# Norm gain moved into the row transposes, small softmax work moved behind the slot table, TensorE order fixed in the route

## The chip, the cores and the metric

One core of one Trainium2 chip. The time is the device time of one execution in microseconds (us): median 3249.14 of 3 runs before the change (3241.06 to 3254.65). TensorE does the matmuls, VectorE, ScalarE and GpSimd the elementwise work, SyncE (SP) issues most DMAs. In the profile PE is TensorE, PEld its weight loads, DVE VectorE, ACT ScalarE, POOL GpSimd.

## The reference, cut to what matters

Two transformer blocks on 1024 tokens of width 1024. The first ends with a mixture of experts; the change is in its routing:

```python
h = _rms_norm(x, norm_ffn_g)                      # rows of hf
g_logits = hf @ w_group_router + b_group_router   # 4 groups
g_probs = softmax(g_logits)
g_gate, g_sel = top_k(g_probs, 1)
e_logits = (hf @ w_expert_router + b_expert_router)[chosen group]   # 8 experts
e_probs = softmax(e_logits)
e_gate, e_sel = top_k(e_probs, 2)
e_gate = e_gate / sum(e_gate)
weights = g_gate * e_gate
# each token goes to 2 of 32 experts; tokens are sorted into slots by expert
hidden = silu(xb @ w_gate[e]) * (xb @ w_up[e])    # xb = hf[tok], the rows of one block of slots
y = (hidden @ w_down[e]) * wt
```

Since the last division cancels the expert softmax's own sum, only the ratio of the two chosen exponentials and the chosen group's share of the group sum enter the weights.

## The kernel before, in words

Activations lie transposed: eight tiles `self.xs[c]` of 128 features by 1024 tokens. Products that need precision run as three passes in the fast 32-bit format (`mm3`, L114 to L116, on high and low parts split by L91 and L94); a few small ones run as plain f32 matmuls, which the hardware carries out as two instructions each (L1004, L1116), and transposes, one instruction each, against the identity matrix.

The first block's cross attention ends with `out(512)` (L735 to L742). Behind it, for each half of 512 tokens, `moe_logits` (L996) computes the norm's reciprocal root and the router's 36 logits per token (L1004, L1009, L1011, L1012), and `moe_rows` (L1015) makes token rows: for each of four blocks of 128 tokens it transposes eight 128x128 pieces (L1023) into two PSUM banks, ScalarE evicts each bank with the token's reciprocal root as scale (L1024), GpSimd multiplies the row by the norm's weights, which `grow` holds copied to all partitions (L1025), and SP writes it to `hrow` in DRAM (L1026). In the text, `moe_rows(0)` stands between the two `moe_logits`, and `moe_rows(512)` behind `route` (L1036, L1037).

`route` (L779) runs almost wholly on VectorE, with instructions of 8 to 256 elements a partition: group softmax (`softmax_small`), first maximum with its one-hot (`first_max`), the logits of the chosen group, expert softmax, two maxima, the weights `wt`, the one-hots `of`, and their sum `both`. TensorE counts positions (L812 with a strictly triangular matrix, then eight matmuls of ones, L815), VectorE picks each token's place, and `turn` (L841) turns token numbers into a slot table per expert by 16 small matmuls against one-hots of the place (L845, L847). `tix` (L832) is the table as integers. Then come expert numbers and counts for `route_rest` (L849), which is called at the third expert and treats experts with more than 112 tokens.

The experts follow: `expert_in` gathers the slots' rows from `hrow` with an indirect DMA from GpSimd (L934), which needs `tix` and all of `hrow`, transposes them (L939) and multiplies with the expert's weights (three loads of 1 MB each on SP, L1047, 12 buffers); `expert_out` makes the second product and writes it to `yrow` (L1060).

The order on each engine isn't that of the text: a planner goes through the program with simulated times and puts what is ready, earliest in the text first. So before the change rows of the second half run on TensorE ahead of the route's own matmuls. `manual_schedule(engines={PE})` makes one region's TensorE instructions issue in the order of the text; where they fall among instructions outside the region stays with the planner. `warm(n)` (L118) issues n matmuls of 512 columns whose result nobody reads; it is used elsewhere in the kernel (L1135 to L1155).

Of the kernel before, what the change touches and what calls it, by code (L numbers as in the profile page):

```python
# [22 lines left out]
P = 128  # L23
S = 1024
D = 1024
# [40 lines left out]
class K:  # L66
# [51 lines left out]
    def warm(self, n):  # L118

        c = self.c  # L120
        ps = self.ps("S", (P, S), 2)[:, 0:512].rearrange("p (r q) -> p r q", q=P)
        for _ in range(n):
            self.nc.tensor.matmul(ps, c["identr"], c["nmaskr"][:, None, :].to_broadcast([P, 4, P]), start=True, stop=True)
# [643 lines left out]
    def softmax_small(self, pool, l, n, tag):  # L767
        nc = self.nc
# [5 lines left out]
        nc.vector.tensor_reduce(mx, p, axis=AX.X, op=OP.add)  # L774
        nc.vector.reciprocal(mx, mx)
        nc.vector.tensor_tensor(p, p, mx.to_broadcast([P, NB, n]), op=OP.mult)
        return p

    def route(self, pool, rp, lg):  # L779
# [15 lines left out]
        den = self.t(rp, [P, NB, 1], tag="den")  # L795
        V.tensor_tensor(den, pk[0], pk[1], op=OP.add)
        V.reciprocal(den, den)
        wt = self.t(pool, [P, NB, 2], tag="wt")
        for k in range(2):
            V.tensor_tensor(wt[:, :, k:k + 1], pk[k], den, op=OP.mult)  # L800
            V.tensor_tensor(wt[:, :, k:k + 1], wt[:, :, k:k + 1], gg, op=OP.mult)
# [11 lines left out]
        for t in range(NB):  # L813
            n = NB - t
            nc.tensor.matmul(ps[:, (t + 1) * 32:].rearrange("p (t e) -> p t e", e=32), self.onesr, both[:, t:t + 1].to_broadcast([P, n, 32]), start=False, stop=(t == NB - 1))  # L815
        pos = ps[:, :256].rearrange("p (t e) -> p t e", e=32)
# [6 lines left out]
        for k in range(2):  # L823
# [6 lines left out]
            self.turn(rp, ps, k, places[k], cols, F32R)  # L830
        tix = self.t(pool, [CAP, 32], I32, tag="tix")
        V.tensor_copy(tix, ps)  # L832

        experts, counts = self.t(pool, [P, 2, NB], tag="experts"), self.t(pool, [P, 32], tag="counts")
        V.tensor_copy(counts, total)
        for k in range(2):
            V.scalar_tensor_tensor(experts[:, k], gv[:, :, 0], 8.0, ev[k][:, :, 0], op0=OP.mult, op1=OP.add)
# [132 lines left out]
    def moe_open(self):  # L970
# [13 lines left out]
        self.grow = self.t(hp, [P, D], tag="grow")  # L984
        nc.sync.dma_start(self.grow, a["norm_ffn_g"].partition_broadcast(P))
# [29 lines left out]
    def moe_rows(self, t0):  # L1015

        nc, hp = self.nc, self.moeh
        for i in range(4):
            row = self.t(self.moeh, [P, D], tag="row", bufs=3)
            for q in range(2):  # L1020
                tp = self.ps("T")
                for n in range(4):
                    nc.tensor.transpose(tp[:, n * P:(n + 1) * P], self.xs[4 * q + n][:, t0 + i * P:t0 + (i + 1) * P], self.c["ident"])  # L1023
# [966 lines left out]
```

## Time and profile before

| | before |
|---|---|
| median of 3 runs | 3249.14 us |
| profiled execution | 3258.15 us, its span 3255.6 us |
| mean granted TensorE clock | 0.967 of full |
| TensorE busy | 3033.3 us, 93% |
| TensorE weight loads | 2447.2 us, 75% |
| VectorE busy | 1618.8 us, 50% |
| ScalarE busy | 1449.5 us, 45% |
| GpSimd busy | 1117.5 us, 34% |
| the chain that ended last | TensorE 53%, every other engine and DMA 1% or less |

Times in the rows below are microseconds from the span's start. A timeline row gives start, length (of a merged group, from its first start to its last end), engine, line, operation, output<-inputs, sizes and count, and in brackets how long the engine had been idle and what ended that. The granted clock is a share of full speed; its two levels are 1.2 and 2.4 GHz, 0.50 and 1.00.

### The profile page before, as it was taken

To read this page: it belongs to the slowest core of one execution; us is meant where nothing else is said; L and a number is where in the kernel's file an instruction comes from. 1 tells how busy PE (TensorE), PEld (TensorE's weight loads), DVE (VectorE), ACT (ScalarE), POOL (GpSimd) and SP (SyncE) were. 2 spreads that over 40 slices of the span, in tenths; PEclk is the share of its full clock that TensorE was granted. 3 is DMA by queue.
4 is the path that set the end of the run, shared out by engine and by line. 5 is a ranking of instruction groups with operands and counts; after the bars stand their busy time and mean duration, and the time that the engine had idled before them with its cause. 6 is when DMAs were issued, how large, how long until landed. Compare 5 with 4: busy or idle time off the path is not lost.

```text
span 3255.6 us, 41825 instructions
## 1 busy us (share of the span) xinstructions
PE 3033.3 (93%) x14660; PEld 2447.2 (75%) x14660; DVE 1618.8 (50%) x3295; ACT 1449.5 (45%) x2906; POOL 1117.5 (34%) x914
## 2 busy tenths in 40 slices
PE   6999779988988999899999999999899999999999
PEld 4787657776756666677888888888777788888887
DVE  6567985577468888663445464331555311111111
ACT  4555664563537888632444453444434221121121
POOL 3334445654533433441111111112656322222221
PEclk9998878999998999999999999999999999999999
DMA  5553636422267999435453333325653211111112
GB/s 161 214 201 125 237 122 197 109 66 85 64 246 270 387 381 356 167 117 153 126 163 123 114 114 104 115 95 197 202 172 112 67 46 47 48 49 43 48 46 81
DMA packets 213003, 469.34 MB, mean 144 GB/s; under 512 B 27544, under 2 KB 69048, under 8 KB 200504
## 3 DMA queue, kind: packets, MB, share of 16 engines
q1 hardware_dynamic: 206392, 443.59, 41.2%
q0 software_dynamic: 6400, 23.07, 2.2%
q8 instruction: 116, 1.90, 0.2%
q14 instruction: 95, 0.78, 0.1%
HBM read 352.28 MB, written 113.77 MB: 143 GB/s over the span
## 4 chain that ended last, share of the span: by engine, by line
PE 53%; DMA 1%; DVE 1%; POOL 1%; ACT 1%; issue 1%; SPq 0%; ACTq 0%; POOLq 0%; DVEq 0%
PE mm L114 16%; PE mm L115 16%; PE mm L116 16%; PE T L1249 1%; PE T L1229 1%; PE S L1477 1%; POOL wlo L94 1%; PE T L1729 0%; PE mm L172 0%; PE T L1710 0%; DMA gt<-gd 0%; PE S L1571 0%; PE S L1570 0%; POOL yg L1100 0%; DMA yg<-yrow,sloti 0%
## 5 line engine op out<-in xcount | busy, mean ns | idle before, releaser
L94 POOL TENSOR_TENSOR wlo<-wraw,whi 128x512 fp32r<-128x512 f32 (+3 forms) x487 | 611.9, 1260 | 1475.7 <-ACT whi L91 1382.8
L115 PE MATMUL mm<-hl,whi 128*128 128x512 f32 (+2 forms) x1968 | 786.5, 400 | 12.0 <-DVE hl L94 6.5
L114 PE MATMUL mm<-hh,whi 128*128 128x512 f32 (+2 forms) x1968 | 787.3, 401 | 10.5 <-DVE qkl L217 2.1
L116 PE MATMUL mm<-hh,wlo 128*128 128x512 f32 (+2 forms) x1968 | 785.0, 399 | 0.0
L91 ACT CAST whi<-wraw 128x512 fp32r<-128x512 f32 (+3 forms) x487 | 287.1, 594 | 712.2 <-PE mm L115 616.8
L115 PEld LDWEIGHTS mm<-hl,whi 128*128 128x128 f32 (+2 forms) x1968 | 371.9, 189 | 100.6 <-DVE hl L94 9.8
L114 PEld LDWEIGHTS mm<-hh,whi 128*128 128x128 f32 (+2 forms) x1968 | 371.7, 189 | 99.3 <-issue 5.0
L116 PEld LDWEIGHTS mm<-hh,wlo 128*128 128x128 f32 (+2 forms) x1968 | 371.7, 189 | 83.2
L94 POOL TENSOR_TENSOR ptl<-praw,pth 128x512 fp32r<-128x512 f32 (+2 forms) x192 | 205.8, 1075 | 235.1 <-DVE pth L1239 200.0
L91 ACT CAST whi<-w 128x512 fp32r<-128x512 f32 x384 | 232.8, 624 | 49.3 <-PE mm L116 18.7
L94 DVE TENSOR_TENSOR wlo<-w,whi 128x512 fp32r<-128x512 f32 x320 | 239.2, 776 | 29.2 <-ACT whi L91 26.1
L1867 DVE TENSOR_TENSOR ffgate<-ffgate,mm 128x512 f32<-128x512 f32 x44 | 30.2, 687 | 384.4 <-PE mm L116 384.4
L1229 PE MATMUL T<-ident,p 128*128 128x128 f32 x864 | 147.4, 291 | 20.5 <-DVE p L450 7.3
L94 POOL TENSOR_TENSOR wlo<-w,whi 128x512 fp32r<-128x512 f32 x64 | 88.6, 1385 | 201.7 <-ACT whi L91 137.3
L1878 DVE TENSOR_TENSOR x<-mm,x 128x512 f32<-128x512 f32 x64 | 44.2, 692 | 199.1 <-PE mm L116 199.1
L1229 PEld LDWEIGHTS T<-ident,p 128*128 128x128 f32 x864 | 107.5, 149 | 44.5 <-ACT praw L1238 9.0
L114 PE MATMUL mm<-ah,whi 128*128 128x512 f32 x352 | 139.6, 397 | 0.3 <-DVE x L1878 0.3
L115 PE MATMUL mm<-al,whi 128*128 128x512 f32 x352 | 139.6, 396 | 0.0
L116 PE MATMUL mm<-ah,wlo 128*128 128x512 f32 x352 | 139.5, 396 | 0.0
L94 DVE TENSOR_TENSOR ptl<-T,pth 128x512 fp32r<-128x512 f32 (+2 forms) x128 | 73.2, 578 | 120.7 <-ACT pth L91 88.9
L1238 ACT COPY praw<-T 128x512 f32<-128x512 f32 (+2 forms) x192 | 90.4, 478 | 82.4 <-PE T L1229 63.5
L444 DVE CUSTOM_DVE_ANT_0 p<-S,dist 128x128 f32<-128x128 f32 (+7 forms) x128 | 94.9, 750 | 40.5 <-PE S L443 32.4
(496 smaller groups left out, 5774.4 us busy)
## 6 DMA issues: line engine op xcount, KB each, us to landing
w<-w_expert SPq DMA_DIRECT2D x96, 1024.0 KB, 10.1
wraw<-w_in SPq DMA_DIRECT2D x152, 256.0 KB, 2.8
gd<-gate SPq DMA_DIRECT2D x64, 256.0 KB, 2.0
gt<-gd SPq DMA_DIRECT2D x16, 1024.0 KB, 6.4
yrow<-y SPq DMA_DIRECT2D x32, 448.0 KB, 3.1
wraw<-w_gate SPq DMA_DIRECT2D x48, 256.0 KB, 2.5
wraw<-w_up SPq DMA_DIRECT2D x48, 256.0 KB
vd<-vs SPq DMA_DIRECT2D x18, 512.0 KB, 2.8
```

What stands on the lines that cost most here:

```text
L91: self.nc.scalar.copy(out, x)
L94: (eng or self.nc.vector).tensor_tensor(out, x, h.bitcast(F32), op=OP.subtract)
L114: self.nc.tensor.matmul(out, lh, rh, start=(i == 0), stop=False)
L115: self.nc.tensor.matmul(out, lh, rl, start=False, stop=False)
L116: self.nc.tensor.matmul(out, ll, rh, start=False, stop=(i == n - 1))
L444: V.tensor_tensor_reduce(p[:, :nk], sps[:, :nk], dist[qb], slope, 3e38, OP.add, OP.min, st[:, m:m + 1])
L1229: nc.tensor.transpose(tp[:, i * P:(i + 1) * P], p[:, (k0 + i) * P:(k0 + i + 1) * P], self.c["ident"])
L1238: nc.scalar.copy(y, src)
L1249: nc.tensor.matmul(o[:, q0:256], vs[:, kb], pt[kb // 4][:, kb % 4, q0:256], start=(pt is pth and kb == 0), stop=(pt is ptl and kb == nkb - 1))
L1477: self.nc.tensor.matmul(o, q, k[:, k0:k0 + kn], start=(i == 0), stop=(i == 1))
L1867: nc.vector.tensor_tensor(g, g, ps, op=OP.mult)
L1878: nc.vector.tensor_tensor(self.xs[i][:, sl], ps, self.xs[i][:, sl], op=OP.add)
```

## The change

`softmax_small` no longer divides by its sum. The group's sum is taken in `route` after the slot table, the sum of the two chosen exponentials is multiplied with it, and one reciprocal gives both weights. These instructions, the copy of the counts and the expert numbers get an edge that lets them issue on VectorE only behind the cast to `tix`. In `moe_rows` the transposes become matmuls with `gdiag`, eight diagonal matrices with the norm's weights, built by GpSimd in `moe_open` in place of the load of `grow`; GpSimd's multiply goes. `route` and `moe_rows(512)` stand in a region in which TensorE issues in the order of the text, with warm matmuls at five places: 10 behind the position matmuls, 6 behind each turn, 14 before the rows and 24 behind them.

```diff
-    def warm(self, n):
+    def warm(self, n, behind=False):
...
-        for _ in range(n):
-            self.nc.tensor.matmul(ps, c["identr"], c["nmaskr"][:, None, :].to_broadcast([P, 4, P]), start=True, stop=True)
+        for i in range(n):
+            m = self.nc.tensor.matmul(ps, c["identr"], c["nmaskr"][:, None, :].to_broadcast([P, 4, P]), start=True, stop=True)
+            if i == 0 and behind:
+                self.tc.keep_in_program_order(m)
...
     def softmax_small(self, pool, l, n, tag):
...
         nc.scalar.activation(p, p, AF.Exp)
-        nc.vector.tensor_reduce(mx, p, axis=AX.X, op=OP.add)
-        nc.vector.reciprocal(mx, mx)
-        nc.vector.tensor_tensor(p, p, mx.to_broadcast([P, NB, n]), op=OP.mult)
         return p
...
     def route(self, pool, rp, lg):
...
-        den = self.t(rp, [P, NB, 1], tag="den")
-        V.tensor_tensor(den, pk[0], pk[1], op=OP.add)
-        V.reciprocal(den, den)
-        wt = self.t(pool, [P, NB, 2], tag="wt")
-        for k in range(2):
-            V.tensor_tensor(wt[:, :, k:k + 1], pk[k], den, op=OP.mult)
-            V.tensor_tensor(wt[:, :, k:k + 1], wt[:, :, k:k + 1], gg, op=OP.mult)
...
+        self.warm(10)
         pos = ps[:, :256].rearrange("p (t e) -> p t e", e=32)
...
             self.turn(rp, ps, k, places[k], cols, F32R)
+            self.warm(6)
         tix = self.t(pool, [CAP, 32], I32, tag="tix")
-        V.tensor_copy(tix, ps)
+        last = V.tensor_copy(tix, ps)
+
+        def behind(x):
+
+            self.tc.add_manual_dep(x.ins, last.ins.name, mybir.DependencyInfo(mybir.DependencyClass.NoSync, mybir.DependencyReason.DATA), reason="behind")
+
+        den, gsum = (self.t(rp, [P, NB, 1], tag=t) for t in ("den", "gsum"))
+        behind(V.tensor_reduce(gsum, gp, axis=AX.X, op=OP.add))
+        behind(V.tensor_tensor(den, pk[0], pk[1], op=OP.add))
+        V.tensor_tensor(den, den, gsum, op=OP.mult)
+        V.reciprocal(den, den)
+        V.tensor_tensor(den, den, gg, op=OP.mult)
+        wt = self.t(pool, [P, NB, 2], tag="wt")
+        for k in range(2):
+            V.tensor_tensor(wt[:, :, k:k + 1], pk[k], den, op=OP.mult)
...
-        V.tensor_copy(counts, total)
+        behind(V.tensor_copy(counts, total))
         for k in range(2):
-            V.scalar_tensor_tensor(experts[:, k], gv[:, :, 0], 8.0, ev[k][:, :, 0], op0=OP.mult, op1=OP.add)
+            behind(V.scalar_tensor_tensor(experts[:, k], gv[:, :, 0], 8.0, ev[k][:, :, 0], op0=OP.mult, op1=OP.add))
...
-        self.grow = self.t(hp, [P, D], tag="grow")
-        nc.sync.dma_start(self.grow, a["norm_ffn_g"].partition_broadcast(P))
+
+        self.gdiag = self.t(hp, [P, 8, P], tag="gdiag")
+        nc.gpsimd.tensor_tensor(self.gdiag, self.c["ident"][:, None, :].to_broadcast([P, 8, P]), self.c["gains"][:, col:col + n, None].to_broadcast([P, 8, P]), op=OP.mult)
...
-                    nc.tensor.transpose(tp[:, n * P:(n + 1) * P], self.xs[4 * q + n][:, t0 + i * P:t0 + (i + 1) * P], self.c["ident"])
+                    nc.tensor.matmul(tp[:, n * P:(n + 1) * P], self.xs[4 * q + n][:, t0 + i * P:t0 + (i + 1) * P], self.gdiag[:, 4 * q + n], start=True, stop=True)
...
-            nc.gpsimd.tensor_tensor(row, row, self.grow, op=OP.mult)
...
-            with tc.tile_pool(name="moer", bufs=1) as rp:
+            with tc.tile_pool(name="moer", bufs=1) as rp, tc.manual_schedule(engines={PE}):
                 tix, rest = self.route(self.moep, rp, self.lg)
+                self.warm(14)
                 self.moe_rows(512)
+                self.warm(24, True)
             self.hes.close()
```

## Rows read from the trace of the kernel before

**Rows 1.** Busy time by windows: start:end, length, engines with counts, PEclk, DMA share, GB/s.
```profile
915.00:930.00 15.00, 15.00 (x82) 12.80 (x81) 8.69 (x19) 6.34 (x12) 6.31 (x4) 1.00 0.52 195
...
960.00:965.00 5.00, 0.14 (x2) 0.00 (x0) 4.36 (x12) 0.23 (x1) 2.85 (x2) 0.93 1.03 397
965.00:970.00 5.00, 0.00 (x0) 0.00 (x0) 4.33 (x20) 0.77 (x2) 0.00 (x0) 0.50 0.85 343
...
990.00:995.00 5.00, 5.00 (x17) 3.70 (x17) 3.52 (x11) 2.30 (x4) 0.93 (x1) 0.50 0.32 99
```

**Rows 2.** Timeline, 955 to 1000 us: the chain through TensorE to the first expert.
```profile
959.49 0.66 PE L1023 MATMUL T<-ident,x 128*128 128x128 f32 x4 [0.20 <-ACT row L1024]
...
973.88 0.61 PE L812 MATMUL mm<-both,stri 128*128 128x288 f32 x1 [13.74 <-DVE both L808]
...
974.29 1.72 PE L815 MATMUL mm<-both,onesr 128*128 128x256 f32 x8
...
978.91 1.68 PE L847 MATMUL mm<-cols,po 128*112 128x32 f32 x8 [1.10 <-DVE cols L829]
...
983.85 0.19 DVE L832 CAST tix<-mm 112x32 int32<-112x32 f32 x1 [1.23 <-PE mm L847]
...
984.93 1.13 POOL L934 DMA_INDIRECT xg<-hrow,tix  x1 [3.87 <-DVE ge L887]
...
989.79 1.73 PE L939 MATMUL T<-ident,xg 112*128 112x112 f32 x8 [5.97 <-DMA xg<-hrow,tix]
```

**Rows 3.** Timeline, 948 to 983 us: VectorE's instructions beside GpSimd's multiply, and two alone.
```profile
950.08 0.31 DVE L1012 TENSOR_TENSOR lg<-lg,br 128x144 f32<-128x144 f32 x1
...
958.46 2.19 DVE L1012 TENSOR_TENSOR lg<-lg,br 128x144 f32<-128x144 f32 x1
...
960.90 1.99 DVE L772 TENSOR_TENSOR gsp<-lg,gsm 128x32 f32<-128x32 f32 x1
...
966.34 0.23 DVE L772 TENSOR_TENSOR esp<-el,esm 128x64 f32<-128x64 f32 x1
...
970.88 2.59 POOL L1025 TENSOR_TENSOR row<-row,grow 128x1024 f32<-128x1024 f32 x1 [8.04 <-ACT row L1024]
971.16 2.34 DVE L838 TENSOR_SCALAR experts<-experts 128x16 f32<-128x16 f32 x1
...
979.32 1.77 DVE L827 SCALAR_TENSOR_TENSOR within<-place,tok 128x8 f32<-128x8 f32 x1
```

**Rows 4.** Timeline: the group softmax's sum, and what follows its product.
```profile
963.19 0.18 DVE L774 TENSOR_REDUCE gsm<-gsp 128x8 f32<-128x32 f32 x1 [0.29 <-ACT gsp L773]
...
963.87 0.19 DVE L757 TENSOR_REDUCE gm<-gsp 128x8 f32<-128x32 f32 x1
```

**Rows 5.** Timeline: prices of transposes, plain f32 matmuls and warm matmuls on TensorE.
```profile
920.71 1.04 PE L1023 MATMUL T<-ident,x 128*128 128x128 f32 x8
...
940.80 7.06 PE L1004 MATMUL mm<-x,wr 128*36 128x512 f32 x16
...
1342.38 14.28 PE L123 MATMUL S<-nmaskr,identr 128*128 128x512 f32 x55 [2.18 <-issue]
...
1362.49 1.84 PE L1116 MATMUL mm<-sqg,sq 128*128 128x2 f32 x16
```

**Rows 6.** Timeline of GpSimd where the router's weights are scaled.
```profile
861.15 0.67 POOL L983 TENSOR_TENSOR wr<-wr,gains 128x288 f32<-128x288 f32 x1 [2.70 <-DMA wr<-w_router]
```

**Rows 7.** One eviction of half a row, and the writes to hrow: first and last start.
```profile
940.47 0.69 ACT L1024 ACTIVATE row<-T,rsr 128x512 f32<-128x512 f32 x1
...
L1026 SPq DMA_DIRECT2D hrow<-row x8: 320/326/327, 928.7 to 981.1; - x8
```

**Rows 8.** Timeline of SP: first, third and fourth output of the experts.
```profile
1011.91 0.33 SPq L1060 DMA_DIRECT2D yrow<-y  x1
...
1035.10 0.33 SPq L1060 DMA_DIRECT2D yrow<-y  x1
...
1045.47 0.33 SPq L1060 DMA_DIRECT2D yrow<-y  x1
```

## The prediction

> **What bounds the kernel now.** I read the windows first. TensorE is full before the route (915 to 930 us), stands still inside it, where the clock falls (960 to 965) to half (965 to 970), and works at half clock when the experts begin (990 to 995) [rows 1]. So the change is worth what it does to one stretch, from the last products before the route to the first expert. Next I read the timeline of that stretch. The chain is: logits, a string of small VectorE instructions, the position matmuls at 973.88, two turns (the first at 978.91), the slot table at 983.85, the first gather at 984.93, the first expert's transposes at 989.79 [rows 2]. From there experts follow each other, so I take a shift of that last point as a shift of the end. The reader is to see that nothing else bounds these 30 us: VectorE works on, TensorE waits for it.
>
> The sum is made against the profiled execution's 3258.15 us (span 3255.6 and 2.55 around it), which is 9.0 above the median of 3249.14; I carry the difference over to the median.
>
> **Part 1, GpSimd's multiply goes.** While GpSimd multiplies a row by the norm's weights, a VectorE instruction that reads SBUF through two inputs, or a tensor_scalar, ends only when GpSimd ends: L1012 took 2.19 us beside a GpSimd pair, and 0.31 alone; L772 1.99 against 0.23 [rows 3]. L838 took 2.34 beside the multiply at 970.88 and L827 1.77; both are smaller than that L772, so 0.23 is their bound alone, and 2.1 and 1.5 go. (L838 isn't in the chain, but the chain's next instruction, L808, stood behind it.) Gone before the position matmuls: 1.88 + 1.76 + 2.1 = 5.7 us; behind them 1.5 us. Nothing else of GpSimd stands in this stretch until the gather.
>
> **Part 2, softmax sums and weights move.** Sum, reciprocal and product took 963.87 - 963.19 = 0.68 us of the chain [rows 4], and there are two such groups: 1.4 us. The weight and expert-number instructions ran in the gaps between dependent ones, so I give them nothing beyond L838 above. Behind the slots they take some 2 us of VectorE, while it would wait for the gather; if that cover is gone they delay route_rest, which nobody waits for at that time.
>
> So the position matmuls move by -7.1 us from this alone.
>
> **Part 3, rows as products with a diagonal.** A transpose costs TensorE 1.04 / 8 = 0.13 us [rows 5]. A plain f32 matmul is two instructions: the router's eight calls are 16, 7.06 us for 512 columns, which is 0.88 a call and 0.22 for a quarter of the columns; 16 instructions with a 128x128 weight and two columns took 1.84, so 0.23 a call is spent on loading alone [rows 5]. No row shows 128 columns with a 128-wide weight. If loads and columns overlap it is 0.23 a call, if they don't 0.23 + 0.22 = 0.45. I take 0.23, as transposes overlap them. Below 0.22 it can't be.
> The first four token rows (32 calls) stand among the products before the route, where TensorE is full [rows 1]: 32 x 0.10 = +3.2 us, on the path; if only part of that work is on it, less, down to 0. Position matmuls begin at 973.88 - 7.1 + 3.2 = 970.0.
> The Trainium skill's "TensorE: Matmul & The Clock Gate" (section Terms) calls the transpose mode four times faster for f32; by that a plain call would be estimated at 4 x 0.13 = 0.52 us, and the sum at 18.6 us more (64 x 0.29), which is 3273 and the first rival's side; the trace's 0.88 for 512 columns speaks for a factor of two at 128.
>
> The diagonal itself is a GpSimd product of 128x1024, 2.4 us by the multiply that is removed [rows 3], in the stage where the router's weights are scaled. GpSimd had 2.70 us idle just before that instruction [rows 6], so 0, at most +2.4 where something there waits for GpSimd; one DMA of SP goes in return.
>
> **Part 4, TensorE in a fixed order.** Now the four rows of the second half come behind both turns, and warming matmuls stand between. In order from 970.0:
> position matmuls, 2.1 us [rows 2]; ten warm ones. 55 of them took 14.28, 0.26 each [rows 5], twice that at half clock. TensorE has idled for long, so it starts at half clock; in the trace the clock is back some 5 us after work resumes (989.79 to about 995) [rows 1, 2]. About six warm ones at 0.5 and four at 0.26 make 4.0: the first turn may begin 6.1 behind the start. VectorE would have it ready at 978.91 - 973.88 = 5.0, so the fillers cost 1.1. The turn itself falls from 1.68 to 0.9. Six more, 1.5 us; VectorE, without the stall, is ready by then; the second turn 0.9. That ends 9.4 behind the start, at 979.4, and the slot table stands at 979.6, where it stood at 984.04: 4.4 us sooner.
> But hrow isn't complete. Behind the turn come 6 + 14 warm matmuls, 20 x 0.25 = 5.0 us, then 32 calls x 0.23 = 7.4 us: rows end on TensorE at 991.8. ScalarE's last eviction takes 0.69 [rows 7], 0.9 with its waits: 992.7. Before, the last row was handed to SP at 981.1 and the gather began at 984.93 [rows 2, 7]: 3.8 us, so the gather begins at 996.5; from gather to transposes 989.79 - 984.93 = 4.9: 1001.4. That is **11.6 us later than before**. What is late next is therefore the row write, which in the old order was overlapped with VectorE's string.
> ScalarE's queue holds only the rows in that stretch, and SP's the row writes; behind the gather on GpSimd stand only gathers and later expert splits.
>
> **Given back behind it.** The last 24 warm matmuls (6 us) reach to 997.8, and 3.6 us of idling before 1001.4 should leave the clock up: in the old trace TensorE's last row ended at 960.15 [rows 2], and the clock still averaged 0.93 from 960 to 965, so it fell only after some 4 us [rows 1]. The first expert then runs at full clock: the 5 us of 990 to 995 [rows 1] become 2.5, -2.5. VectorE's route_rest ran among the first experts; the third output left 1035.10 - 1011.91 = 23.2 us after the first, where the steady pitch is 1045.47 - 1035.10 = 10.4 [rows 8], 2.4 more than two pitches. Now it fits into the wait for rows: -2.4, and perhaps -1 within the first expert. Together -6. Bounds: 0 and -8.
>
> **Sum**: +11.6 - 6 = +5.6 us: 3264 for a profiled execution, **3255 as median**. Lower end with the first half's 3.2 us off the path and -8 given back: +0.4; upper with nothing given back and +2.4 for the diagonal: +14.
>
> **Rivals.**
> *Plain matmuls cost twice what I take.* At 0.45 a call (load and columns in series) the 64 calls cost 0.22 x 64 = 14 us more, all on the path: 3269. It becomes slower beyond 0.5% (which is about what a measurement of this kernel tells from none, 16 us) from 0.40 a call (10.6 / 64 on top of 0.23). For it: no such row; against it: both parts were seen to overlap in transposes and in the router's matmuls.
> *The rows hide.* Should the rows of the second half be done by the time of the slot table (placed early, or the fillers running much faster than reckoned), the gather begins at 979.6 + 0.9, the transposes at 985.4, 4.4 sooner, and with 6 given back: 3239; with the first half's rows hidden too, 3236; with the bound of -8, 3234. For it: rows of the second half did run before the position matmuls in the old order [rows 2]. Against: the region lets TensorE issue in the order of the text, and there the rows stand last.
> *The clock stays low.* If the fillers don't raise it, 20 fillers and 32 calls run at half speed: +5.6 + 5 + 7.4, and the first expert's 2.5 isn't gained: 3270. It decides if TensorE stays at 0.50 for 5 us behind the position matmuls. Against it: from there on TensorE has no gap of a microsecond.
> *The planner orders something else differently.* It plans by simulated times, and these change at the route; a weight load that comes to stand one expert later costs up to a pitch of 10.4 [rows 8], one that stands sooner can save it: 3245 or 3265 with one, 3234 or 3276 with two. Nothing in the profile speaks for a direction.
>
> **How the numbers follow.** Forecast 0.58 (own range 3249 to 3263), all of it within 0.5%. First and third rival together 0.15, of which 0.11 is slower. Rows hide 0.13, of which 0.07 faster. Planner 0.14: 0.05 faster, 0.05 slower. Faster 0.12, same 0.72, slower 0.16. The range takes in all but the tails of the rivals: 3237 to 3270.
>
> **What would show it.** Right, if no VectorE instruction of the route lasts over 1 us, the position matmuls begin some 7 us sooner counted from the last logits' product, the slot table is ready well before the gather, and the gather waits for a row write some 16 us behind the table; if L1023 shows 128 instructions at about 0.115; if the clock is 1.00 when the first transposes begin. Wrong, if rows run ahead of the turns, if a plain call takes over 0.3 us, if the clock is at half in the rows, or if the distance from the first expert's output to the end changes by more than 3 us.

## The result, and the profile after

The changed kernel takes 3267.04 us (median of 6 runs) against 3250.14 (6 runs of before beside it): ratio 1.0051, interval 1.0038 to 1.0064. It is 17 us slower, at the edge of the 0.5% that a measurement tells from no change. The forecast was 3255, its range 3237 to 3270: the time lies inside, 12 us above the forecast and 3 below the upper end.

| | after |
|---|---|
| profiled execution | 3260.81 us, its span 3259.0 us |
| mean granted TensorE clock | 0.974 of full |
| TensorE busy | 3041.8 us, 93% |
| TensorE weight loads | 2453.7 us, 75% |
| VectorE busy | 1612.2 us, 49% |
| ScalarE busy | 1450.4 us, 45% |
| GpSimd busy | 1097.0 us, 34% |
| the chain that ended last | TensorE 53%, VectorE 2%, others 1% or less |

The windows of the changed kernel that answer to [rows 1] (start:end, length, engines with counts, PEclk, DMA share, GB/s):

```profile
960.00:965.00 5.00, 0.00 (x0) 0.00 (x0) 4.24 (x18) 0.26 (x1) 0.00 (x0) 0.56 1.00 362
965.00:970.00 5.00, 3.87 (x14) 3.48 (x15) 2.65 (x8) 0.00 (x0) 0.00 (x0) 0.50 0.13 52
970.00:975.00 5.00, 5.00 (x31) 4.30 (x30) 3.33 (x10) 0.00 (x0) 0.00 (x0) 0.91 0.00 0
990.00:995.00 5.00, 2.70 (x12) 1.89 (x11) 4.18 (x23) 0.00 (x0) 2.41 (x2) 0.98 0.30 95
995.00:1000.00 5.00, 3.75 (x13) 2.97 (x14) 2.82 (x7) 1.51 (x3) 0.92 (x1) 0.50 0.37 101
1000.00:1005.00 5.00, 5.00 (x24) 3.85 (x24) 4.98 (x22) 3.63 (x8) 0.93 (x1) 0.84 0.29 86
```

The fillers bring the clock back by 970 to 975, and it is still 0.98 at 990 to 995; then it is at half again, just where the first expert begins.

Its timeline answers to [rows 2, 3, 5]. L805 and L808 are the position matmuls, L123 the fillers, L856 a turn, L827 the slot table, L1033 the rows, L868 the begin of `route_rest`, L943 the gather, L948 the first expert's transposes:

```profile
957.74 0.31 DVE L1021 TENSOR_TENSOR lg<-mm,rsr 128x144 f32<-128x144 f32 x1 [5.99 <-PE mm L1019]
958.08 0.31 DVE L1022 TENSOR_TENSOR lg<-lg,br 128x144 f32<-128x144 f32 x1
958.65 0.19 DVE L775 TENSOR_TENSOR gsp<-lg,gsm 128x32 f32<-128x32 f32 x1
966.13 0.61 PE L805 MATMUL mm<-both,stri 128*128 128x288 f32 x1 [8.43 <-DVE both L801]
968.09 3.84 PE L123 MATMUL S<-nmaskr,identr 128*128 128x512 f32 x10
971.77 0.87 PE L856 MATMUL mm<-cols,po 128*112 128x32 f32 x8
973.96 0.87 PE L856 MATMUL mm<-cols,po 128*112 128x32 f32 x8
974.67 4.81 PE L123 MATMUL S<-nmaskr,identr 128*128 128x512 f32 x20
974.86 0.19 DVE L827 CAST tix<-mm 112x32 int32<-112x32 f32 x1 [1.42 <-PE mm L856]
979.33 7.90 PE L1033 MATMUL T<-gdiag,x 128*128 128x128 f32 x64
986.98 5.71 PE L123 MATMUL S<-nmaskr,identr 128*128 128x512 f32 x24
987.26 0.69 ACT L1034 ACTIVATE row<-T,rsr 128x512 f32<-128x512 f32 x1 [0.15 <-PE T L1033]
990.71 0.46 DVE L868 TENSOR_TENSOR nov<-counts,caps 128x288 f32<-128x288 f32 x1 [14.45 <-DMA hrow<-row]
991.50 1.13 POOL L943 DMA_INDIRECT xg<-hrow,tix  x1 [50.17 <-DVE ge L896]
996.25 1.73 PE L948 MATMUL T<-ident,xg 112*128 112x112 f32 x8 [3.56 <-DVE rtmp L902]
```

VectorE's stalls are gone: L1022 and L775 take 0.31 and 0.19 where L1012 and L772 took 2.19 and 1.99. The slot table stands 17.1 us behind the logits (25.7 before), but the gather comes 16.6 us behind the table (1.1 before): it waits for the rows, which end 12 us behind the table.

SP's first, second and third expert output ([rows 8] have first, third and fourth):

```profile
1018.39 0.33 SPq L1071 DMA_DIRECT2D yrow<-y  x1
1031.22 0.33 SPq L1071 DMA_DIRECT2D yrow<-y  x1
1041.59 0.33 SPq L1071 DMA_DIRECT2D yrow<-y  x1
```

From first to third 23.2 us, as before.

**Reading by stretch.** Two executions of one program differ more than the change is worth: a second trace of before has a span of 3244.0 us, 11.6 under the first. But they differ in other stretches. I cut each trace at four points: the last instruction that reads `mo` (756.1 in before, ahead of all that the change touches), the second half's logits (L1021), the first expert's transposes (L948), the first and the last expert's output (the start of its eviction `y` on ScalarE). In the four stretches between these, the two traces of before agree within 0.2 us, and so do two traces of the changed kernel, save the second (0.6). From the last output to the end it is 1908.4 and 1915.3 us in the two traces of before, and 1908.2 to 1916.0 over all kernels here, so nothing of the change shows there. So the stretches show what a total hides, with one caution: the other ten kernels have one trace each. In the table, "sum" is their change against before, and "timed" the difference of the medians. The last column is one wait of TensorE inside the last stretch, of which more below.

| kernel | to logits | to first expert | to its output | to last output | sum | timed | wait for `xh` |
|---|---|---|---|---|---|---|---|
| before (two traces) | 202.0 | 31.6 | 21.05 | 329.35 | | | 9.8 |
| changed (two traces) | 204.85 | 38.8 | 21.05 | 333.45 | +14.2 | +15.4, +16.9 | 13.2, 13.3 |
| rows first | 206.2 | 28.5 | 20.3 | 329.1 | 0.0 | +5.0 | 9.0 |
| no fill before rows | 204.9 | 34.2 | 22.3 | 331.3 | +8.8 | +8.9 | 10.8 |
| planner order | 206.1 | 26.1 | 21.1 | 333.9 | +3.1 | +3.0 | 10.5 |
| rest's memory first | 204.9 | 38.5 | 20.6 | 330.0 | +10.0 | +11.6 | 8.9 |
| half on GpSimd | 203.5 | 25.9 | 21.1 | 327.7 | -5.9 | -5.8 | 8.3 |
| softmax only | 203.5 | 29.3 | 20.9 | 332.3 | +2.0 | 0.0 | 11.3 |
| four row buffers | 204.9 | 25.7 | 19.9 | 333.2 | -0.3 | +1.8 | 11.4 |
| long fill | 204.9 | 38.5 | 19.4 | 330.1 | +8.9 | +14.3 | 9.0 |
| hybrid filled | 204.9 | 25.7 | 20.0 | 335.0 | +1.6 | +5.8 | 15.1 |
| ScalarE's queue | 203.5 | 28.3 | 20.3 | 328.6 | -3.4 | -1.5 | 8.3 |

The sum is within 2.1 us of the timed difference (2.7 for the first measurement of the changed kernel) but for three kernels (rows first, long fill, hybrid filled: 4 to 5.5 short); what these lose elsewhere stays open.

Some single traces hold 3.4 us at half clock that the traces of before and of the changed kernel don't have there. In softmax only, four row buffers and hybrid filled they lie in the cross attention, some 108 us behind the first cut, and make "to logits" 1.5 us longer. In no fill before rows, planner order, softmax only and long fill they lie at the last expert and make "to last output" 1.2 to 1.6 us longer. Softmax only has both:

```profile
865.00:870.00 5.00, 4.63 (x26) 4.63 (x27) 2.42 (x6) 2.77 (x12) 2.51 (x3) 0.66 0.10 38
1340.00:1345.00 5.00, 3.68 (x10) 2.18 (x8) 0.00 (x0) 1.01 (x1) 0.00 (x0) 0.66 0.05 19
```

Why the clock fell there stays open.

### The profile page after: what moved, and what is told of

Its sections match the earlier page's. It is cut to its first block, busy times and chain, and to the rows that moved or that the text cites. A ratio compares the mean times of both kernels' runs of the same rounds, so it can differ in the third digit from the quotient of the medians.

```text
span 3259.0 us, 42063 instructions
## 1 busy us (share of the span) xinstructions
PE 3041.8 (93%) x14784; PEld 2453.7 (75%) x14784; DVE 1612.2 (49%) x3290; ACT 1450.4 (45%) x2906; POOL 1097.0 (34%) x907
## 4 chain that ended last, share of the span: by engine, by line
PE 53%; DVE 2%; DMA 1%; POOL 1%; ACT 1%; issue 0%; SPq 0%; ACTq 0%; POOLq 0%; DVEq 0%
PE mm L114 16%; PE mm L115 16%; PE mm L116 15%; PE T L1260 1%; PE T L1240 1%; PE S L1488 1%; POOL wlo L94 1%; PE T L1740 0%; PE mm L174 0%; PE T L1721 0%; DMA gt<-gd 0%; PE S L1582 0%; DVE gt L1817 0%; PE T L1118 0%; PE S L1581 0%
## 5 line engine op out<-in xcount | busy, mean ns | idle before, releaser
L114 PE MATMUL mm<-whi,xh 128*112 128x512 f32 x256 | 104.3, 407 | 13.2 <-ACT xh L91 13.2
## 6 DMA issues: line engine op xcount, KB each, us to landing
w<-w_expert SPq DMA_DIRECT2D x96, 1024.0 KB, 10.1
```

The lines of the kernel that those rows point to most:

```text
L114: self.nc.tensor.matmul(out, lh, rh, start=(i == 0), stop=False)
```

## The experiments

**Changed kernel again.** No edit.

> The changed kernel once more, nothing edited. Both theories: 3267 within 4 us. From the second half's logits (the VectorE product that scales them) to the first expert's transposes 38.5 us, within 0.3, as in its first trace; from those transposes to the span's end 2262.7, and how far that moves in a second trace of the same program says what a single trace can tell there.

3267.19 us, ratio 1.0048 (1.0033 to 1.0063) against 3251.83. The size is confirmed, and so is the last stretch: 333.4 after 333.5. Logits to first expert is not quite what was expected: 39.1 us, 0.6 above the first trace.

**Rows first.**

```diff
+                self.moe_rows(512)
                 tix, rest = self.route(self.moep, rp, self.lg)
-                self.warm(14)
-                self.moe_rows(512)
-                self.warm(24, True)
+                self.warm(18, True)
```

> Token rows of the second half stand before the route in the region (14 fillers dropped, the last 24 cut to 18). Theory A, the late rows set the first expert's start and the end follows one to one: rows fit into VectorE's string of 8 us, the gather begins about 1 us behind the slot table, logits to first transposes 23 to 27 us in place of 38.5, and the time falls by 11 to 15 us to 3252 to 3256. Theory B, the time was lost to other orders that the planner chose behind the experts: the start moves, the end doesn't follow, 3262 to 3272. Theory C, plain matmuls are dear: the position matmuls move out by as much as the rows take beyond 8 us, and less than half of the gain is left, 3260 or more.

3256.8 us, ratio 1.0010 (1.0001 to 1.0019): 10.4 us better than the changed kernel with every other part of it in place, save 20 fillers. Logits to first expert fall from 38.8 to 28.5. The late rows, with the fillers ahead of them, were the price. But rows that come early meet the weights' prefetch; its timeline:

```profile
976.90 1.27 ACT L1034 ACTIVATE row<-T,rsr 128x512 f32<-128x512 f32 x2 [3.69 <-DMA hrow<-row]
977.64 3.48 PE L1033 MATMUL T<-gdiag,x 128*128 128x128 f32 x16 [5.46 <-ACT row L1034]
980.88 0.38 PE L805 MATMUL mm<-both,stri 128*128 128x288 f32 x1
988.35 0.18 DVE L827 CAST tix<-mm 112x32 int32<-112x32 f32 x1
990.17 0.16 DVE L841 TENSOR_TENSOR wt<-e1m,den 128x8 f32<-128x8 f32 x1
991.31 1.14 POOL L943 DMA_INDIRECT xg<-hrow,tix  x1 [40.71 <-DVE ends L877]
```

ScalarE waits 3.69 us for a row buffer that a write still holds, TensorE waits 5.46 for ScalarE, and in the fixed order the position matmuls stand behind it. That write is the first half's last: issued at 958.5 beside the weights' loads, it landed at 976.8. The second half's last write, issued at 981.9, landed in 2.6 us; by the slot table's end (988.53) all rows were there. Yet the gather began 2.8 us behind the table, where before it was 0.9. It began 1.0 us behind the last of the weights `wt`, which the change moved behind the table; "four row buffers" comes back to this.

**No fill before rows.**

```diff
-            self.warm(6)
+            if k == 0:
+                self.warm(6)
...
-                self.warm(14)
                 self.moe_rows(512)
```

> Only the 6 fillers behind the second turn and the 14 before the rows are taken out; the rows follow the second turn at once. Theory A: rows, gather and first transposes come 4.8 us sooner (20 fillers x 0.23 us + waits), logits to first transposes 33.7, time 3262. Theory B: the time moves by anything within 6 us, not by the start's amount. If the clock falls because fillers are missing, the rows take up to twice 7.9 us and nothing is gained: 3267 or more.

3260.72 us, ratio 1.0034 (1.0020 to 1.0047): -6.5 against the changed kernel. The first expert starts 4.6 us sooner behind the logits, nearly the 4.81 that the 20 fillers took. Fillers ahead of work that is on the path cost almost their whole length.

**Planner order.**

```diff
-        self.warm(10)
...
-            self.warm(6)
...
-            with tc.tile_pool(name="moer", bufs=1) as rp, tc.manual_schedule(engines={PE}):
+            with tc.tile_pool(name="moer", bufs=1) as rp:
                 tix, rest = self.route(self.moep, rp, self.lg)
-                self.warm(14)
                 self.moe_rows(512)
-                self.warm(24, True)
```

> Region and all fillers of the route are taken out; the diagonal products and the moved softmax work stay. Theory A: the planner again places rows of the second half ahead of the position matmuls, where TensorE waits, logits to first transposes 23 to 28 us, the turns and the first expert at half clock cost 2 to 4 us against the rows-first form, time 3252 to 3258. Theory B: 3262 to 3272. Theory C: as for the rows-first form, 3260 or more.

3254.79 us, ratio 1.0009 (1.0000 to 1.0019). Parts 1 to 3 alone bring the first expert 5.6 us nearer to the logits than before, and yet the time is 3 us above: 4.1 go ahead of the logits, where the plain matmuls stand, and 4.5 among the experts, 1.6 of them at the last one's half clock.

**Before again.** No edit; one trace.

> The kernel before once more, unchanged, for a second trace of it: it sizes what a single trace may be off. If the lengths of stages are the program's, the stage from the first expert's output to the last's is 329.3 us again, as in the first trace, against 333.5 and 333.4 in the two traces of the changed kernel, and the stretch from the logits to the first expert's transposes 31.7 us. If they are noise of the single trace, the expert stage comes out anywhere between 328 and 334.

Single time 3246.5 us. Logits to first expert 31.6, first to last output 329.4: these lengths belong to the program. The 11.6 us between the spans arose elsewhere: 4.5 ahead of the first cut, and 6.9 behind the last output.

**The rest's memory first.** `route_rest`'s pool is opened ahead of the experts' pool.

```diff
+            lp = es.enter_context(tc.tile_pool(name="moel", bufs=1))
             ep = es.enter_context(tc.tile_pool(name="moee", bufs=2))
             self.nunit = 0
-            lp = es.enter_context(tc.tile_pool(name="moel", bufs=1))
```

> The changed kernel, with the memory of the third routing step (L868 and on) opened ahead of the experts' own, so that it no longer lies where the row buffers were. Theory A (in the changed kernel this step waited for the last rows' writes, 990.7 instead of some 976, and so gave nothing back behind the first expert): the step begins before 980, the pitch from the first to the third expert output falls from 23.2 to 20 to 21 us, and the time comes to 3264.5, -2.5 against the changed kernel's 3267.2. Rival B (the experts' own loads and splits fill that time whatever VectorE does ahead of it): the pitch stays 23.2 and the time 3267.

3262.46 us, ratio 1.0036 (1.0023 to 1.0049), some 4 better than the changed kernel, but not for the reason given. The wait goes, as its timeline shows:

```profile
980.54 0.16 DVE L841 TENSOR_TENSOR wt<-e1m,den 128x8 f32<-128x8 f32 x1
980.74 0.46 DVE L868 TENSOR_TENSOR nov<-counts,caps 128x288 f32<-128x288 f32 x1
```

VectorE's part of `route_rest` begins straight behind the weights, 20 us ahead of the first transposes (1000.7). Still the third output follows the first by 22.95 us instead of 23.2. So theory A falls on its own number: VectorE's `route_rest` is not what makes these pitches long. TensorE's part is, as far as the traces show: the two turns of `route_rest` are 32 small instructions on TensorE, which in every kernel here run between the first output and the second, however early VectorE begins. In this run, the instructions, the first pitch and the second:

```profile
L856 PE MATMUL mm<-ocols,po x32: 193/266/266, 1021.4 to 1029.4; 128*112 128x36 f32 x32
1022.36:1034.95 12.59, 12.59 (x77) 10.07 (x77) 11.18 (x22) 9.63 (x18) 3.52 (x3) 1.00 0.98 312
1034.95:1045.31 10.36, 9.60 (x47) 7.05 (x46) 9.11 (x14) 9.06 (x18) 4.44 (x3) 1.00 1.02 357
```

TensorE is busy throughout the first, 3.0 us more than in the second; in before it is 12.69 of 12.83 us, then 9.60 of 10.36. No run moved these instructions. What this run gained, 3.5 us, lies in the last stretch behind the tenth expert.

**Half on GpSimd.** Planner order, with the first half's rows as before.

```diff
+        self.grow = self.t(hp, [P, D], tag="grow")
+        nc.sync.dma_start(self.grow, a["norm_ffn_g"].partition_broadcast(P))
...
+                    x = self.xs[4 * q + n][:, t0 + i * P:t0 + (i + 1) * P]
+                    if t0:
-                    nc.tensor.matmul(tp[:, n * P:(n + 1) * P], self.xs[4 * q + n][:, t0 + i * P:t0 + (i + 1) * P], self.gdiag[:, 4 * q + n], start=True, stop=True)
+                        nc.tensor.matmul(tp[:, n * P:(n + 1) * P], x, self.gdiag[:, 4 * q + n], start=True, stop=True)
+                    else:
+                        nc.tensor.transpose(tp[:, n * P:(n + 1) * P], x, self.c["ident"])
...
+            if not t0:
+                nc.gpsimd.tensor_tensor(row, row, self.grow, op=OP.mult)
```

> The changed kernel in the planner's own order (no fillers, as in the run with planner order, 3254.8), with the first half of the rows as before: transposes and the multiply on GpSimd; only the second half has the matmuls with the weights. Theory C (in the changed kernel the first half's plain matmuls stand on TensorE's path ahead of the logits, where nothing hides them: norm to logits 204.9 to 206.2 us against 202.0): norm to logits is 202 to 203 again, and the time falls by 3 to 4 us to 3251 (3249.5 to 3252.5), which is that of before or a little under. Rival B (the 3 us above before come from the experts' stage, which the planner orders otherwise): 3254.8, no change.

3245.07 us, ratio 0.9987 (0.9978 to 0.9996): the one kernel here that beats both, by 5.8 and some 22 us, though 5.8 is still inside the 0.5%; theory C had given it less. Against planner order, 2.6 us come back to the logits and 6.1 among the experts. (The 1.5 that remain above before are calls of the second half that stand ahead of the logits: TensorE's rows there take 7.7 us instead of 6.2.) Theory C's gain is there (203.5 to the logits, where it had 202 to 203); the rest of the gain is the experts' stage, which neither theory had on that side.

**Softmax only.** Before, with the second part alone (the diff of `softmax_small` and `route`, without fillers).

```diff
-        V.tensor_copy(tix, ps)
+        last = V.tensor_copy(tix, ps)
...
-        nc.vector.tensor_reduce(mx, p, axis=AX.X, op=OP.add)
-        nc.vector.reciprocal(mx, mx)
-        nc.vector.tensor_tensor(p, p, mx.to_broadcast([P, NB, n]), op=OP.mult)
```

> The kernel before, with the second part of the change alone: softmax sums and weights behind the slots. By the prediction's own term (-1.4 us of VectorE ahead of the position matmuls) the first expert starts 1.4 to 2 us sooner and the time is 3250.2 against 3251.8. Rival: GpSimd's multiplies, which stay, stall VectorE by as much as it gains (the stalls of 2 us move to other instructions): 3251.8, no change. Second rival: the planner orders the experts otherwise, as it did with the whole change (+4 us in that stage): 3254.

3250.87 us against 3250.88, ratio 1.0000 (0.9991 to 1.0009). The position matmuls come 3.7 us sooner behind the logits (12.1 against 15.8), the first expert 2.3, since the gather now begins 2.2 us behind the table instead of 0.9. The last stretch takes 2.95 back, as the second rival has it, with less; but 1.6 of that is half clock at the last expert. Another 1.5 go ahead of the logits, where the edit touches nothing; they are half clock too, in the first of the two windows shown above. GpSimd's multiply, kept here, still holds VectorE's instructions:

```profile
961.54 2.20 DVE L1017 TENSOR_TENSOR lg<-lg,br 128x144 f32<-128x144 f32 x1
963.99 1.99 DVE L773 TENSOR_TENSOR gsp<-lg,gsm 128x32 f32<-128x32 f32 x1
```

**Four row buffers** (on half on GpSimd).

```diff
-            row = self.t(self.moeh, [P, D], tag="row", bufs=3)
+            row = self.t(self.moeh, [P, D], tag="row", bufs=4)
```

> The run with half the rows multiplied on GpSimd (3245.1) with four row buffers instead of three. There the last two evictions of rows waited 5.08 us for a row buffer whose write stood behind the weight loads, the last write was issued at 971.2, and the first gather began at 976.2, 3.2 us behind the slot table. Theory D (the row buffers make the last rows late): the evictions end by 962, the gather starts within 0.5 us of the slot table, the first transposes come 2 to 3 us sooner and the time is 3242.5. Rival E (the writes themselves are slow beside the weight loads, whoever issues them): the last write is issued sooner, lands at the same time, and the time stays 3245.

3250.76 us against 3248.96, ratio 1.0004 (0.9992 to 1.0015). Half of theory D holds: the last write goes out 11.4 us behind the logits instead of 15.4, and has landed 3.0 us ahead of the slot table's end (976.0 and 979.04), though one eviction still waits 5.2 us, for the first half's last write, 21.2 us under way. The other half doesn't: the gather still starts 3.0 us behind the slot table. The rows weren't what it waited for:

```profile
978.86 0.18 DVE L825 CAST tix<-mm 112x32 int32<-112x32 f32 x1
980.68 0.16 DVE L839 TENSOR_TENSOR wt<-e1m,den 128x8 f32<-128x8 f32 x1
981.91 1.13 POOL L941 DMA_INDIRECT xg<-hrow,tix  x1 [35.15 <-DVE ends L875]
```

In all seven kernels that have `wt` behind the table and the rows in time (rows first, planner order, half on GpSimd, softmax only, this one, hybrid filled, ScalarE's queue), the gather starts 0.97 to 1.07 us behind the end of the last `wt`, while that lies anywhere from 1.2 to 3.2 us behind the table. In each trace GpSimd's wait on VectorE's semaphore ends 0.04 us after that `wt`. So the gather waits for the moved instructions, which compute nothing that it reads. A likely reason is that the experts' buffers take over the memory of the route's small tiles; no run tests that. The time lost against half on GpSimd, 5.5 us, is in the last stretch, whose code wasn't touched.

**Long fill** (on the changed kernel).

```diff
-                self.warm(24, True)
+                self.warm(40, True)
```

> The changed kernel with 40 instead of 24 fillers behind the last rows, so that TensorE is busy until some 996.5, when the first gather has landed. It tests the prediction's term of the clock. Theory F (in the changed kernel the granted clock had fallen to 0.50 again by 995, so the first expert ran at half clock; at full clock it is 2.5 us shorter): the windows of 995 to 1005 have a clock near 1.00, from the first transposes to the first output 18.5 instead of 21.0 us, and the time is 3264.7, -2.5. Rival G (the first expert is bound by the splits on ScalarE and VectorE and by the return of weight buffers, not by TensorE): clock 1.00, the stretch 20.5 to 21, the time 3267; or, if the fillers outlast the gather, up to 1 us more.

3263.25 us, ratio 1.0043 (1.0029 to 1.0056). Fillers reach the first transposes and the clock stays:

```profile
985.00:990.00 5.00, 5.00 (x32) 4.39 (x31) 0.00 (x0) 1.81 (x3) 0.00 (x0) 1.00 0.64 256
990.00:995.00 5.00, 5.00 (x24) 4.14 (x23) 4.72 (x25) 0.00 (x0) 2.42 (x2) 1.00 0.36 103
995.00:1000.00 5.00, 4.72 (x25) 3.24 (x24) 4.49 (x17) 2.77 (x5) 0.93 (x1) 1.00 0.50 159
```

First transposes to first output: 19.4 instead of 21.0. Full clock is worth 1.6 us there, between F's 2.5 and G's 0.5 (hybrid filled, with 3.4 us at half clock behind its first transposes, lies between, at 20.0); the pitch to the third output stays 23.2.

**Hybrid filled** (rows first, first half on GpSimd, four row buffers, fillers ahead of the position matmuls too).

```diff
                 self.moe_rows(512)
+                self.warm(16)
                 tix, rest = self.route(self.moep, rp, self.lg)
-                self.warm(18, True)
+                self.warm(24, True)
```

> What the runs so far speak for, put together: the first half of the rows as before (GpSimd's multiply, far ahead of the routing), the second half's matmuls with the weights ahead of the routing in TensorE's order, four row buffers, 16 fillers until the position matmuls, then the changed kernel's own fillers (10, 6, 6, 24). Theory A (the end follows the start of the first expert): norm to logits 203.5, logits to first transposes 24 to 25 us (31.7 before, 38.6 changed), the time 3241 to 3243. Rival (fillers or the fixed order hold something else up, or the experts' stage falls out long, as it did in two other orders, +4): 3247, no better than without them (3245.1).

3254.76 us, ratio 1.0019 (1.0010 to 1.0028). Theory A's route comes about in part (25.7 us to the first expert, 5.9 less than before, where it had 24 to 25; VectorE puts `route_rest` between, so the last `wt` ends 3.2 us behind the table), the rival's price too: the last stretch is 335.0, the longest of all.

**ScalarE's queue** (on half on GpSimd).

```diff
-            nc.sync.dma_start(self.hrow[t0 + i * P:t0 + (i + 1) * P, :], row)
+            (nc.scalar if t0 else nc.sync).dma_start(self.hrow[t0 + i * P:t0 + (i + 1) * P, :], row)
```

> The run with half the rows multiplied on GpSimd (3245.1), with the second half's row writes issued from ScalarE's queue, behind their evictions, instead of SyncE's, where nine weight loads stand ahead of them (writes there took up to 20.7 us to land, and the last two evictions waited 5.1 us for a row buffer). Theory H (a write waits in its queue behind the weight loads): from another queue it lands within 5 us, the evictions have no wait for a buffer, the first gather starts within 0.5 us of the slot table instead of 3.2 behind it, logits to first transposes 23 instead of 26.0 us, and the time is 3242. Rival E (the transfer engines are full, DMA share 1.0, and every queue waits alike): landing 10 us and more, first transposes unchanged, 3245. With either, the experts' stage can come out up to 5 us longer by the planner's order (327.7 to 335.0 so far); then the stretch from the logits to the first transposes decides.

3250.18 us against 3251.63, ratio 0.9994 (0.9984 to 1.0004). None of theory H's signs comes. Its timeline of row writes and of ScalarE, and its windows:

```profile
948.30 0.33 SPq L1041 DMA_DIRECT2D hrow<-row  x1
958.01 0.35 ACTq L1041 DMA_DIRECT2D hrow<-row  x1
960.36 0.33 ACTq L1041 DMA_DIRECT2D hrow<-row  x1
970.49 1.27 ACT L1038 ACTIVATE row<-T,rsr 128x512 f32<-128x512 f32 x2 [7.03 <-DMA hrow<-row]
```

```profile
960.00:965.00 5.00, 1.54 (x13) 1.27 (x11) 3.75 (x16) 0.70 (x3) 0.00 (x0) 1.00 1.02 385
965.00:970.00 5.00, 2.13 (x9) 2.02 (x9) 2.61 (x11) 0.00 (x0) 0.00 (x0) 0.67 0.68 269
```

But the run doesn't test the theory where the wait is. The write that holds the row buffer until 970.4 is the first half's last, issued at 948.3 on SP, as without the edit: 22.1 us. The two writes that the edit does move beside the loads, issued at 958.0 and 960.4 with the transfer engines full (DMA share 1.02), landed after 8.5 and 9.2 us; from SP's queue, in half on GpSimd, the same two took 11.7 and 10.6. So a queue of its own took 1.4 to 3.2 us off a write; rival E's 10 us and theory H's 5 both miss. (The Trainium skill's "DMA: Bandwidth & Descriptors", section Queues, rings and completion order, has each transfer engine take turns packet by packet between the queues it has work for; by that a write from its own queue needn't wait for all the loads ahead of it. The direction agrees with this run; no run has the first half's last write on such a queue.) Logits to first transposes are 28.3 us, 2.3 longer: rows stand ahead of the turns on TensorE and wait for that buffer, so the slot table comes 2.4 us later, and the gather again 1.06 behind `wt`.

## Why the prediction was right or wrong

By stretches, the forecast's +11.6 - 6 came out as +10.1, 0 and a +4.1 that it did not have. The time lies above the forecast's own range (3249 to 3263). It is inside 3237 to 3270 only because that range was widened for rivals that did not come about: plain calls at twice the price, and a clock at half through the rows (it was 1.00 there). What took their place, the experts' stage, had no share in the sum. That part is luck.

**Right: the way to the first expert.** Position matmuls behind the logits: -7.1 predicted, 15.8 to 8.4 measured, -7.4. Plain matmuls ahead of the logits: +3.2 predicted, +2.85 measured. (At the end of the first half's 32 calls TensorE is 3.7 us later than before; 0.9 comes back up to the logits, since 13 transposes of the second half that ran there before now come late.) The diagonals' product took GpSimd 1.90 us, from 853.4 on, and up to the first rows, at 917.4, TensorE keeps step with before within some 0.2 us, so it cost nothing. A plain call took 7.90 / 32 = 0.247 us, where 0.23 was taken and 0.45 was the upper bound. The Trainium skill's "TensorE: Matmul & The Clock Gate" (Terms) has the transpose four times faster; against 0.13 a call it is 1.9 times here, so that rival's price falls and the measurement decides. Ten fillers took 3.84 (4.0), the second turn ended 8.7 us behind the position matmuls' begin (9.4), the last row write to the gather took 3.5 (3.8), the gather to the transposes 4.75 (4.9). The first expert starts 2.85 + 7.2 = 10.1 us later; +11.6 was predicted. "Rows hide" is borne out against the changed kernel (rows first and planner order give 10 and 12 us back), but not against before: it had 3239, they take 3256.8 and 3254.8, with 4.1 ahead of the logits, the gather held by `wt` and nothing given back.

**Wrong: "Given back behind it", -6.** Measured 0: first transposes to first output 21.0, first to third output 23.2, as before. Both reasons failed.
- The clock. The fillers ended at 992.7, and TensorE idled 3.56 us, the 3.6 of the prediction; the clock was 0.98 at 990 to 995 and 0.50 at 995 to 1000. The prediction had inferred from [rows 1, 2] that it would stay up. With it up, the long fill shows 1.6 us, not 2.5: so the 5 us of half clock in [rows 1] were not TensorE's alone. That the splits on ScalarE and VectorE beside it make the difference is argued.
- `route_rest`. It did not fit into the wait for rows: it waited 14.45 us for their last write and began at 990.71. That its memory lay where the row buffers had been is shown by the run that moves it. But that run also shows that the long pitch behind the first output is not VectorE's: with its part begun 20 us ahead, it gives 0.25 us of the 2.4. The prediction had taken the wrong engine: the first pitch is 12.6 to 12.8 us in every kernel here, and TensorE fills it, with the 32 instructions of `route_rest`'s turns.

**Wrong, but without a price here: what stands behind the slots.** Part 2 let the moved instructions delay only `route_rest`. The seven kernels above show that the gather waits for them, up to 3.2 us behind the table. In the changed kernel the rows come later still, so it cost nothing.

**Missed: the experts' stage, +4.1.** The outputs keep step with before up to the tenth (96.4 us in both), then fall back. This is the fourth rival's mechanism at another price: not a weight load that shifts by a pitch, but one wait of TensorE, repeated. TensorE's waits from first to last output (total us, times, longest), in the second trace of before, the changed kernel, half on GpSimd, and hybrid filled:

```profile
PE mm L114 <- ACT xh L91: 9.8, 14, 1.3
```

```profile
PE mm L114 <- ACT xh L91: 13.2, 16, 1.3
```

```profile
PE mm L114 <- ACT xh L91: 8.3, 16, 1.3
```

```profile
PE mm L114 <- ACT xh L91: 15.1, 16, 1.3
```

`xh` is the high part of an expert's gathered rows, cast by ScalarE. Where it stands on ScalarE right behind two casts of weights, TensorE waits 0.37 us in nearly all cases; where one of the two is the eviction of an output (`y`, 1.0 us), 1.28 us: 5 such waits in before, 8 in the changed kernel, 2 in half on GpSimd, 10 in hybrid filled. The table's last column follows the stretch (8.3 at 327.7 and 328.6, 13.2 at 333.5, 15.1 at 335.0; planner order, 10.5 at 333.9, fits badly, also without the 1.6 us of half clock). TensorE's busy time in it stays within 301.4 and 302.5, save planner order (304.3) and softmax only (303.7), which have that half clock. That the wait carries most of the difference, 3.5 of the 4.1 us, is measured; that the planner's simulated times decide the order, and why they tip as they do, is argued. No run fixed ScalarE's order.

So of 14.2 us, 2.85 are plain matmuls ahead of the logits, 7.2 the late rows net of VectorE's gain, and 4.1 the experts' stage, most of it the casts' order; the forecast had the first two and took 6 off for things that did not come.

By the prediction's own list: no VectorE instruction of the route over 1 us, position matmuls 7 us sooner, the gather waiting for the rows: right. Clock 1.00 at the first transposes: wrong. The distance from the first output changed by more than 3 us: this it had named as what would make it wrong.

## What to carry to other kernels

Work that is put behind others in a fixed order is paid for in full if something waits for it: here rows, fillers and row writes put 21.4 us between slot table and first transposes, where 5.9 had been, to save 8.6 ahead of it, while the planner's own order kept that gain (slot table 17.1 us behind the logits) and added 3.0. Work that is moved behind a result can still hold up that result's consumer: look at what the consumer starts behind, not only at what it reads (here the gather starts 1.0 us behind `wt`). Price a saving by the next thing that its consumer needs (the gather needs table and rows), and count nothing as "given back" unless a row shows that the freed time was the limit, and on which engine. Before explaining a few microseconds of total, cut two traces of the same kernel at the same points: the stretches that repeat carry the evidence. And a planner can move an untouched stage by 7 us.

## What the runs showed of the hardware

- A row write landed 2.6 us after its issue with idle transfer engines, and 18 to 22 us after it beside the weights' loads (the first half's last, in every kernel). ScalarE's queue made it 8.5 and 9.2 us instead of 11.7 and 10.6 for two others.
- Half clock behind the first transposes cost 1.6 us, not the 2.5 that the windows suggested.
- Identical programs gave spans 11.6 us apart, with the stretches around the change equal within 0.2 us (0.6 in one stretch of the changed kernel). Single traces had 3.4 us at half clock where others had none, at a price of 1.2 to 1.6 us.
